# A hybrid encoder step on one core: attention's PSUM banks given to the dense products, the last mixer's products reordered, one projection moved from step 20 to step 15

## The chip, the cores and the metric

The kernel runs on one core of one Trainium2 chip. The metric is the device time of that core in microseconds (us). The kernel before takes 3145.21 us, the median of three runs (3145.02 to 3149.61). The profiled execution that all rows below come from took 3148.22 us, of which the program's span is 3146.1 us.

## The reference

One inference step of a two-layer trunk with width 1024: layer 0 has a recurrent mixer, layer 1 has chunk-band softmax attention, and both have a SwiGLU channel mixer behind their layer norm. There are 1088 rows of activations (1024 of the prompt, 64 of a running stream). What matters here is the end of layer 1:

```python
def layer_norm(x, w, b):
    xf = x.astype(F32)
    mu = jnp.mean(xf, -1, keepdims=True)
    var = jnp.mean(jnp.square(xf - mu), -1, keepdims=True)
    return ((xf - mu) * lax.rsqrt(var + LN_EPS) * w.astype(F32) + b.astype(F32)).astype(x.dtype)

def swiglu(x, w_in, w_out):
    gate, up = jnp.split(x @ w_in, 2, axis=-1)
    return (jax.nn.silu(gate) * up) @ w_out
```

Attention gives a head's output from softmax(q k + bias) v, where each row reads its own chunk of 64 rows and the eight chunks before it. Its output goes through a projection, is added to the residual, normalised, and goes through `swiglu` with 2816 hidden columns.

## The kernel before, in words

**Two halves.** The activations are kept as half A (448 columns) and half B (640 columns, done as two times 320). In the last stage of layer 1 three pieces of work overlap: half B's attention, half A's channel mixer, and, after both, half B's output projection and half B's channel mixer, which ends the program.

**Products.** Everything is float32, made on TensorE (PE) from halves: each operand is split into a high part (`xh`, `wh`) and a low part (`xl`, `wl`), and each product is three matmuls (`wh` by `xh`, `wh` by `xl`, `wl` by `xh`; lines L122 to L124 with the weights stationary, L133 to L136 the other way round). A weight tile of 128x1024 is loaded to `wr`; ScalarE (ACT) makes `wh` (L99), and the low part is made in pieces on VectorE (DVE, L104) and GpSimd (POOL, L106).

**PSUM.** PSUM has eight banks here. `bank` (L138) hands out the three that dense products use, as `gps`. From the start of attention, five others belong to the pool `atps`: two for the scores (`sps`, one buffer of two banks) and three with the tag `t` for attention's transposed probabilities (`tp`), its output (`op`) and the layer norm's transposes (`tps`). The pool is held to the end of the program.

**Half B's attention** goes by pairs of heads; a head has five tiles of 128 rows, in a group of three and a group of two. For one tile: scores on PE (L1262, L1263), add of the bias with the row maximum on DVE (L1266), its negation (L1270), exponential on ACT (L1271), reciprocal on DVE (L1272), scaling on POOL (L1273), four or five transposes on PE (L1278), split of the transposed tile by ACT (L1288) and DVE (L1289). After a group, `op` is accumulated on PE (L1304) and joined (L1308, L1309). The buffer `s` that goes from L1266 to L1278 exists twice.

**Half A's mixer** is a generator `f` of 22 steps. A step loads two weight tiles (gate and up), makes two products of 24 matmuls 448 wide, and forms the hidden tile `ht` and its split `hh`, `hl`. After steps 4, 8, 12, 16, 18 and 22 the products with the second weights (512 wide) are added to the residual `acc`. In program order, each of the last six pairs of attention is followed by two steps of `f`; then comes the rest of `f`, into which half B's projection (`proj`, `layer_norm` and `s_operands`, which forms the sums below) is put at step `JM`.

**Half B's mixer** (`s_ffn`) uses seven products of 12 matmuls, 320 wide, for what would be eight: with the operand's quarters A11, A12, A22 and sums S1 to S4, and the weights' B11, B21, B22 and sums T1 to T4. `s_weights` makes the weights' sums on POOL (L1019 to L1024) and splits them on ACT (L1013) and DVE (L1014). The products run from L1039 to L1041; the 22 steps have three PSUM banks in turn, `pa`, `pb` and `pc`.

**Order of the work.** The code is written in program order, and a scheduler then places the instructions on five engine queues, each of which runs in order. It moves work across program order wherever buffers and inputs allow.

Of the kernel before, what the change touches and what calls it, by code (L numbers as in the profile page):

```python
# [9 lines left out]
F32 = mybir.dt.float32  # L10
# [3 lines left out]
ALU = mybir.AluOpType  # L14
PS = bass.MemoryType.PSUM
# [67 lines left out]
class Kern:  # L83
    def __init__(self, ctx, tc, a):
        self.ctx, self.tc, self.nc, self.a = ctx, tc, tc.nc, a
        self.V, self.A, self.G, self.T = self.nc.vector, self.nc.scalar, self.nc.gpsimd, self.nc.tensor
        self.wcount = 0
        self.both = False
        self.paired = False

# [45 lines left out]
                self.T.matmul(ps, cols(lo(kt)), wh, start=False, stop=(i == n - 1))  # L136

    def bank(self):  # L138
        return self.gp.tile([128, 512], F32, tag="g", name="gps", bufs=3)

    def banks(self, hf):
# [886 lines left out]
    def s_ffn(self, layer, acc, x, hp, hidden, turn, after):  # L1028

        V, A, G, T = self.V, self.A, self.G, self.T  # L1030
        hs, done = {}, 0
        for j in range(NHT):
            B = self.s_weights(j, layer, turn)
            pa, pb, pc = (self.bank()[:, :320] for _ in range(3))

            def product(ps, xn, bn, first):
                (xh, xl), (wh, wl) = x[xn], B[bn]
                for kt in range(4):
                    T.matmul(ps, wh[:, kt, :], xh[:, kt, :], start=(first and kt == 0), stop=False, skip_group_check=True)  # L1039
                    T.matmul(ps, wh[:, kt, :], xl[:, kt, :], start=False, stop=False, skip_group_check=True)  # L1040
                    T.matmul(ps, wl[:, kt, :], xh[:, kt, :], start=False, stop=(kt == 3), skip_group_check=True)  # L1041

            def tmp(n, w=320):
                return hp.tile([128, w], F32, tag=n, name=n, bufs=2)

            t = tmp("ht", 640)
            t1, t2 = t[:, :320], t[:, 320:]
            product(pa, "A11", "B11", True)
            c1 = tmp("c1")
            A.copy(c1, pa)  # L1050
            product(pb, "S2", "T2", True)
            c2 = tmp("c2")
            V.tensor_tensor(c2, pb, c1, op=ALU.add)
            product(pc, "S1", "T1", True)
            product(pb, "S3", "T3", False)
            c3 = tmp("c3")
            V.tensor_tensor(c3, pb, c1, op=ALU.add)
            V.tensor_tensor(c3, pc, c3, op=ALU.add)
            product(pa, "A12", "B21", False)
            A.activation(t1, pa, AF.Tanh, scale=0.5)  # L1060
            V.scalar_tensor_tensor(t1, t1, 1.0, pa, op0=ALU.add, op1=ALU.mult)
            product(pc, "S4", "B22", False)
            V.tensor_tensor(c2, pc, c2, op=ALU.add)
            G.tensor_tensor(t1, t1, c2, op=ALU.mult)
            product(pb, "A22", "T4", False)
            V.tensor_tensor(c1, pb, c1, op=ALU.add)
            A.activation(t2, c1, AF.Tanh, scale=0.5)
            V.scalar_tensor_tensor(t2, t2, 1.0, c1, op0=ALU.add, op1=ALU.mult)
            G.tensor_tensor(t2, t2, c3, op=ALU.mult)
            hh, hl = hidden(j)  # L1070
            A.activation(hh, t, AF.Copy, scale=0.5)
            V.scalar_tensor_tensor(hl, t, 0.5, hh.bitcast(F32), op0=ALU.mult, op1=ALU.subtract)
            hs[j] = hh, hl
            end = j + 1
            if end in self.GROUPS:
                self.tsg(1, acc, lambda nh, pr: self.a["w_fo"][layer, nh, pr], range(done // 2, end // 2),
                         lambda kt: hs[kt][0], lambda kt: hs[kt][1], done == 0, after() if end == NHT else None)
                for i in range(done, end):
                    del hs[i]
                done = end  # L1080
# [235 lines left out]
    def run(self):  # L1316
        nc, tc, a = self.nc, self.tc, self.a
# [2 lines left out]
        self.gla_d = self.dp.tile([2, 128, 128], F32, name="gla_d", tag="gla_d")  # L1320
        self.JX = 6
        self.PB, self.QB, self.turn, self.AQ = 1, 2, 0, (1, 4)
        self.HB, self.PRE, self.JO, self.JM = 5, 4, 16, 20
        es_scan, es_one, es_ps = ExitStack(), ExitStack(), ExitStack()
        self.sp_ps = es_ps.enter_context(tc.tile_pool(name="scps", bufs=1, space=PS))
        self.tpsum = lambda: self.sbank("tps")
# [34 lines left out]
        pa = es_a.enter_context(tc.tile_pool(name="accA", bufs=1))  # L1361
# [46 lines left out]
                    acc1 = self.load_acc(1, a["x"], accp)  # L1408
                self.qk(0, hp, qp, 2)
        es_ps.close()  # L1410
        self.at_ps = self.ctx.enter_context(tc.tile_pool(name="atps", bufs=1, space=PS))
        self.tpsum = lambda: self.at_ps.tile([128, 512], F32, tag="t", name="tps", bufs=3)
        self.proj(1, acc1, "w_om", self.layer_norm(1, acc1, "ln1", 0))
        with tc.tile_pool(name="at0", bufs=1, side="right") as atp:
# [15 lines left out]
        with tc.tile_pool(name="at1", bufs=1, side="right") as atp:  # L1430
# [16 lines left out]
            for hp in range(len(self.AQ), 8):  # L1447
                self.attention(1, hp, atp, parts)
                for _ in range(2):
                    next(f)  # L1450
        for j in f:
            if j == self.JM:
                accp = self.ctx.enter_context(tc.tile_pool(name="accB1", bufs=1, side="right"))
# [97 lines left out]
```

## Time and profile before

| What | Value |
|---|---|
| runs | 3145.21 us (3145.02 to 3149.61) |
| profiled execution | 3148.22 us, span 3146.1 us, mean granted PE clock 0.978 |
| PE busy | 3012.1 us (96%) |
| DVE, ACT, POOL busy | 2026.2, 1264.6, 1331.3 us (64, 40, 42%) |
| longest single wait of PE after 2394.5 us | 22.3 us, on L1039 for L975 |
| last 21 attention tiles and the dense products between them | 2394.5 to 2544.0 us |
| rest of half A's mixer, half B's projection | 2544.0 to 2684.3 us |
| half B's mixer | 2684.3 to 3115.0 us |

Rows of the timeline begin with start and duration in us, then engine, line and operation, `out<-in` by the program's names; a number in brackets is the idle time before it and what ended it. Rows of stretches give the length, then busy us and instructions for PE, PE's weight loads, DVE, ACT and POOL, then the granted PE clock, the DMA share and GB/s. Matmuls are pipelined, so the duration of one is about twice the distance from start to start of a run of them; below, matmuls are priced by that distance.

### The profile page before, as it was taken

The page shows a single profiled execution, that of the slowest core. Times are in us where ns is not written, and L with a number is a line of the kernel's source. Part 1 is how long each engine was busy: PE and PEld are TensorE (multiplying, and loading weights), DVE is VectorE, ACT ScalarE, POOL GpSimd, SP SyncE. Part 2 cuts the span into 40 slices and gives each one's busy share as a digit, 9 for nine tenths or more (in the row PEclk, how much of TensorE's full clock was granted, in tenths as well). Part 3 has the DMA queues.
Part 4 walks back from the last instruction along what each step waited for, and adds up shares of the span by engine and source line. Part 5 has one row for each costly group of instructions (what it writes and reads, how often), then busy time and mean ns, then how long its engine had stood idle before and what let it go on. Part 6 is the DMA issues. An engine that isn't in the chain of part 4 may idle for free.

```text
span 3146.1 us, 50008 instructions
## 1 busy us (share of the span) xinstructions
PE 3012.1 (96%) x17468; PEld 2670.6 (85%) x17468; DVE 2026.2 (64%) x4953; ACT 1264.6 (40%) x2753; POOL 1331.3 (42%) x1461
## 2 busy tenths in 40 slices
PE   9989999899999999999999999999999997899998
PEld 7778888688888877888999898899999886798887
DVE  4677885879898664365553556245666659666557
ACT  4454554344445324244342223355444433333322
POOL 2354533445555234343342323244545535445444
PEclk9989999889999999999999999999999998999999
DMA  6553444534533248434333234765545342222122
GB/s 201 142 155 113 111 113 118 149 103 113 142 105 110 84 131 268 153 111 126 115 110 97 74 101 138 239 184 162 148 141 151 115 145 99 86 68 94 63 72 74
DMA packets 297339, 395.09 MB, mean 126 GB/s; under 512 B 125376, under 2 KB 218424, under 8 KB 297088
## 3 DMA queue, kind: packets, MB, share of 16 engines
q1 hardware_dynamic: 297088, 391.90, 41.8%
q8 instruction: 138, 2.26, 0.3%
q14 instruction: 113, 0.93, 0.1%
HBM read 319.44 MB, written 75.51 MB: 126 GB/s over the span
## 4 chain that ended last, share of the span: by engine, by line
PE 73%; DVE 12%; DMA 7%; issue 3%; ACT 2%; POOL 2%; SPq 1%; POOLq 0%; DVEq 0%; ACTq 0%
PE gps L122 11%; PE gps L123 11%; PE gps L124 11%; PE gps L133 7%; PE gps L134 7%; PE gps L136 6%; PE gps L1039 2%; PE op L1304 2%; PE gps L1040 2%; PE gps L1041 2%; PE tp L1278 2%; DVE t L543 1%; DVE wl L104 1%; DVE x L545 1%; PE sps L1262 1%
## 5 line engine op out<-in xcount | busy, mean ns | idle before, releaser
L106 POOL TENSOR_TENSOR wl<-wr,wh 128x512 fp32r<-128x512 f32 (+2 forms) x289 | 506.0, 1755 | 626.5 <-ACT wh L99 580.5
L122 PE MATMUL gps<-xh,wh 128*128 128x320 f32 (+1 forms) x2188 | 748.4, 342 | 10.2 <-ACT xh L209 5.7
L123 PE MATMUL gps<-xl,wh 128*128 128x320 f32 (+1 forms) x2188 | 747.2, 341 | 0.6 <-DVE xl L210 0.6
L124 PE MATMUL gps<-xh,wl 128*128 128x320 f32 (+1 forms) x2188 | 744.1, 340 | 0.7 <-DVE wl L104 0.7
L99 ACT CAST wh<-wr 128x1024 fp32r<-128x1024 f32 x352 | 366.9, 1048 | 458.5 <-PE gps L123 140.8
L122 PEld LDWEIGHTS gps<-xh,wh 128*128 128x128 f32 x2188 | 415.3, 190 | 32.0 <-ACT wh L99 6.0
L104 DVE TENSOR_TENSOR wl<-wr,wh 128x512 fp32r<-128x512 f32 (+2 forms) x289 | 284.5, 985 | 244.0 <-ACT wh L99 239.4
L123 PEld LDWEIGHTS gps<-xl,wh 128*128 128x128 f32 x2188 | 415.2, 190 | 18.7 <-DVE xl L210 1.0
L124 PEld LDWEIGHTS gps<-xh,wl 128*128 128x128 f32 x2188 | 414.9, 190 | 18.4 <-DVE wl L104 1.1
L1273 POOL TENSOR_SCALAR s<-s,mx 128x640 f32<-128x640 f32 (+5 forms) x144 | 203.4, 1413 | 289.9 <-DVE mx L1272 250.0
L133 PE MATMUL gps<-wh,xh 128*128 128x512 f32 x661 | 262.6, 401 | 10.9 <-DVE acc L816 4.0
L136 PE MATMUL gps<-wh,xl 128*128 128x512 f32 x661 | 259.5, 398 | 4.8 <-DVE xl L210 4.8
L134 PE MATMUL gps<-wl,xh 128*128 128x512 f32 x661 | 261.7, 398 | 2.0 <-DVE wl L104 2.0
L133 PE MATMUL gps<-wh,hh 128*128 128x512 f32 x572 | 226.5, 397 | 2.7 <-DVE acc L818 1.4
L134 PE MATMUL gps<-wl,hh 128*128 128x512 f32 x572 | 225.4, 396 | 0.0
L818 DVE TENSOR_TENSOR acc<-acc,gps 128x512 f32<-128x512 f32 (+1 forms) x216 | 144.7, 679 | 85.3 <-PE gps L136 79.8
L136 PE MATMUL gps<-wh,hl 128*128 128x512 f32 x484 | 188.8, 396 | 2.2 <-DVE hl L924 2.2
L543 DVE TENSOR_TENSOR t<-lt,x 16x48 f32<-16x48 f32 (+9 forms) x540 | 151.6, 281 | 38.6 <-DMA lt<-l_d 28.2
L1271 ACT ACTIVATE s<-s,mx 128x640 f32<-128x640 f32 (+5 forms) x144 | 96.5, 670 | 178.6 <-DVE mx L1270 173.3
L133 PEld LDWEIGHTS gps<-wh,xh 128*128 128x128 f32 x661 | 125.0, 189 | 44.6 <-DVE acc L816 4.8
L136 PEld LDWEIGHTS gps<-wh,xl 128*128 128x128 f32 x661 | 125.1, 189 | 32.9 <-DVE xl L210 5.3
L545 DVE TENSOR_TENSOR x<-x,t 16x48 f32<-16x48 f32 (+9 forms) x540 | 144.0, 267 | 10.9
(351 smaller groups left out, 6291.8 us busy)
## 6 DMA issues: line engine op xcount, KB each, us to landing
wr<-in_w_fi SPq DMA_DIRECT2D x176, 512.0 KB
wr<-in_w_fo SPq DMA_DIRECT2D x88, 512.0 KB
wr<-in_w_in SPq DMA_DIRECT2D x44, 512.0 KB
wr<-in_w_qk SPq DMA_DIRECT2D x32, 512.0 KB
qs<-qd SPq DMA_DIRECT2D x32, 320.0 KB
wr<-in_w_om SPq DMA_DIRECT2D x16, 512.0 KB
wr<-in_w_v SPq DMA_DIRECT2D x16, 512.0 KB
vd<-vh SPq DMA_DIRECT2D x16, 512.0 KB
```

The lines of the kernel that those rows point to most:

```text
L99: self.A.copy(hi, raw)
L104: self.V.tensor_tensor(lo[:, :h], raw[:, :h], hi[:, :h].bitcast(F32), op=ALU.subtract)
L106: self.G.tensor_tensor(lo[:, h:], raw[:, h:], hi[:, h:].bitcast(F32), op=ALU.subtract)
L122: self.T.matmul(ps, hi[:, kt, :], xh, start=(kt == 0), stop=False)
L123: self.T.matmul(ps, hi[:, kt, :], xl, start=False, stop=False)
L124: self.T.matmul(ps, lo[:, kt, :], xh, start=False, stop=(kt == nk - 1))
L133: self.T.matmul(ps, xh, wh, start=(i == 0), stop=False)
L134: self.T.matmul(ps, xh, wl, start=False, stop=(lo is None and i == n - 1))
L136: self.T.matmul(ps, cols(lo(kt)), wh, start=False, stop=(i == n - 1))
L543: V.tensor_tensor(tv, lt[:, j, w:16].unsqueeze(2).to_broadcast([m, r, w]), x[:, 0, j, 0:w].unsqueeze(1).to_broadcast([m, r, w]), op=ALU.mult)
L545: V.tensor_tensor(x[:, 0, w:16, 0:w], x[:, 0, w:16, 0:w], tv, op=ALU.add)
L1273: G.tensor_scalar(s[:m, :nk], s[:m, :nk], mx[:m, 3:4], None, op0=ALU.mult)
```

## The change

It has three parts. After the last attention, `atps` is closed and its five banks are opened as a second pool for `bank`, which then alternates three tiles of the old pool with five of the new one; the transposes of the layer norm (`tpsum`) take `bank` too. In `s_ffn` a fourth bank `pd` is used, S2·T2 is written ahead of A11·B11, S3·T3 and A22·T4 go to `pd`, and the sums `c1`, `c2`, `c3` are formed in another order (one copy and five additions per step, as before). `JM` goes from 20 to 15. Line numbers after the change are higher by 1 from `bank` on, and by 5 behind it.

```diff
@@ -84,7 +84,8 @@
     def __init__(self, ctx, tc, a):
         self.ctx, self.tc, self.nc, self.a = ctx, tc, tc.nc, a
         self.V, self.A, self.G, self.T = self.nc.vector, self.nc.scalar, self.nc.gpsimd, self.nc.tensor
-        self.wcount = 0
+        self.wcount = self.bcount = 0
+        self.gp2 = None
         self.both = False
         self.paired = False
 
@@ -136,6 +137,10 @@
                 self.T.matmul(ps, cols(lo(kt)), wh, start=False, stop=(i == n - 1))
 
     def bank(self):
+
+        self.bcount += 1
+        if self.gp2 and self.bcount % 8 > 2:
+            return self.gp2.tile([128, 512], F32, tag="g2", name="gps", bufs=5)
         return self.gp.tile([128, 512], F32, tag="g", name="gps", bufs=3)
 
     def banks(self, hf):
@@ -1031,7 +1036,7 @@
         hs, done = {}, 0
         for j in range(NHT):
             B = self.s_weights(j, layer, turn)
-            pa, pb, pc = (self.bank()[:, :320] for _ in range(3))
+            pa, pb, pc, pd = (self.bank()[:, :320] for _ in range(4))
 
             def product(ps, xn, bn, first):
                 (xh, xl), (wh, wl) = x[xn], B[bn]
@@ -1045,25 +1050,23 @@
 
             t = tmp("ht", 640)
             t1, t2 = t[:, :320], t[:, 320:]
+            c1, c2, c3 = tmp("c1"), tmp("c2"), tmp("c3")
+            product(pb, "S2", "T2", True)
+            A.copy(c1, pb)
             product(pa, "A11", "B11", True)
-            c1 = tmp("c1")
-            A.copy(c1, pa)
-            product(pb, "S2", "T2", True)
-            c2 = tmp("c2")
-            V.tensor_tensor(c2, pb, c1, op=ALU.add)
+            V.tensor_tensor(c1, pa, c1, op=ALU.add)
             product(pc, "S1", "T1", True)
-            product(pb, "S3", "T3", False)
-            c3 = tmp("c3")
-            V.tensor_tensor(c3, pb, c1, op=ALU.add)
-            V.tensor_tensor(c3, pc, c3, op=ALU.add)
+            V.tensor_tensor(c3, pc, c1, op=ALU.add)
+            product(pd, "S3", "T3", True)
+            V.tensor_tensor(c3, pd, c3, op=ALU.add)
             product(pa, "A12", "B21", False)
             A.activation(t1, pa, AF.Tanh, scale=0.5)
             V.scalar_tensor_tensor(t1, t1, 1.0, pa, op0=ALU.add, op1=ALU.mult)
             product(pc, "S4", "B22", False)
-            V.tensor_tensor(c2, pc, c2, op=ALU.add)
+            V.tensor_tensor(c2, pc, c1, op=ALU.add)
             G.tensor_tensor(t1, t1, c2, op=ALU.mult)
-            product(pb, "A22", "T4", False)
-            V.tensor_tensor(c1, pb, c1, op=ALU.add)
+            product(pd, "A22", "T4", False)
+            V.tensor_tensor(c1, pd, c1, op=ALU.add)
             A.activation(t2, c1, AF.Tanh, scale=0.5)
             V.scalar_tensor_tensor(t2, t2, 1.0, c1, op0=ALU.add, op1=ALU.mult)
             G.tensor_tensor(t2, t2, c3, op=ALU.mult)
@@ -1320,7 +1323,7 @@
         self.gla_d = self.dp.tile([2, 128, 128], F32, name="gla_d", tag="gla_d")
         self.JX = 6
         self.PB, self.QB, self.turn, self.AQ = 1, 2, 0, (1, 4)
-        self.HB, self.PRE, self.JO, self.JM = 5, 4, 16, 20
+        self.HB, self.PRE, self.JO, self.JM = 5, 4, 16, 15
         es_scan, es_one, es_ps = ExitStack(), ExitStack(), ExitStack()
         self.sp_ps = es_ps.enter_context(tc.tile_pool(name="scps", bufs=1, space=PS))
         self.tpsum = lambda: self.sbank("tps")
@@ -1408,7 +1411,8 @@
                     acc1 = self.load_acc(1, a["x"], accp)
                 self.qk(0, hp, qp, 2)
         es_ps.close()
-        self.at_ps = self.ctx.enter_context(tc.tile_pool(name="atps", bufs=1, space=PS))
+        es_at = ExitStack()
+        self.at_ps = es_at.enter_context(tc.tile_pool(name="atps", bufs=1, space=PS))
         self.tpsum = lambda: self.at_ps.tile([128, 512], F32, tag="t", name="tps", bufs=3)
         self.proj(1, acc1, "w_om", self.layer_norm(1, acc1, "ln1", 0))
         with tc.tile_pool(name="at0", bufs=1, side="right") as atp:
@@ -1448,6 +1452,9 @@
                 self.attention(1, hp, atp, parts)
                 for _ in range(2):
                     next(f)
+        es_at.close()
+        self.gp2 = self.ctx.enter_context(tc.tile_pool(name="gp2", bufs=1, space=PS))
+        self.tpsum = self.bank
         for j in f:
             if j == self.JM:
                 accp = self.ctx.enter_context(tc.tile_pool(name="accB1", bufs=1, side="right"))
```

The number of instructions on PE (15089 rows), DVE, POOL and SP stays the same. The order of the queues is the same up to the first row shown here. In the following, `gps` is a dense product, `tp`, `sps` and `op` belong to attention; the number behind a name tells buffers apart.

**PE, where the last 21 attention tiles begin.** Before:

```order
L124 MATMUL gps_27101<-xh0_69,wl_27090 128x448
L122 MATMUL gps_27101<-xh0_69,wh_27089 128x448
L1278 MATMUL tp_25674<-ident_71,s_25667 128x128 x4
L1278 MATMUL tp_25681<-ident_71,s_25667 128x128
L123 MATMUL gps_27101<-xl0_70,wh_27089 128x448
L1262 MATMUL sps_25724<-ks_25611,qs_25612 128x320
L1263 MATMUL sps_25724<-ks_25611,qs_25612 128x320
```

Now:

```order
L134 MATMUL gps_27075<-wh_27028,hh_26947 128x512
L135 MATMUL gps_27075<-wl_27029,hh_26947 128x512
L1281 MATMUL tp_25674<-ident_71,s_25667 128x128 x4
L1281 MATMUL tp_25681<-ident_71,s_25667 128x128
L1265 MATMUL sps_25724<-ks_25611,qs_25612 128x320
L1266 MATMUL sps_25724<-ks_25611,qs_25612 128x320
```

Before, dense products of half A's step 12 (counted from 0) stand between the pieces of an attention tile, and so on for the next 760 rows. Now the attention tiles follow one another with no dense product in between.

**PE, where those attention tiles end.** Now:

```order
L1307 MATMUL op_26789<-xh1_23955,vt_26498 128x128
L1307 MATMUL op_26789<-xl1_23956,vt_26498 128x128
L123 MATMUL gps_27105<-xh0_69,wh_27093 128x448
L124 MATMUL gps_27105<-xl0_70,wh_27093 128x448
L125 MATMUL gps_27105<-xh0_69,wl_27094 128x448
```

The dense product `gps_27105` is the one that before was `gps_27101`, in the rows above. It now stands behind the last `op` of attention, and with it everything of half A's steps 12 to 21. Behind it come steps 12 to 15 and their second weights, then half B's projection, then step 16.

**DVE, where half B's normalised rows are made.** These are residual rows `acc`, their splits `xl1`, the sums S2 to S4, and the low half `wl` of half A's next weights. Before:

```order
L818 TENSOR_TENSOR acc_28001<-acc_28001,gps_28440 128x512
L982 TENSOR_TENSOR ss_28331<-sc_28330,st_28332 128x256
L866 BN_STATS bs_28454<-acc_28001 128x6
L104 TENSOR_TENSOR wl_28596<-wr_28593,wh_28595 128x640
L988 TENSOR_TENSOR sc_28330<-tps_28314,sc_28330 128x256
```

Now:

```order
L113 TENSOR_TENSOR xl1_27521<-gps_28028,xh1_27520 128x4x64
L997 TENSOR_TENSOR ss_28045<-gps_28035,ss_28045 128x256
L980 TENSOR_TENSOR st_28120<-xh1_27520,xl1_27521 128x256
L105 TENSOR_TENSOR wl_28159<-wr_28156,wh_28158 128x640
L823 TENSOR_TENSOR acc_27566<-acc_27566,gps_28065 128x512
```

Before, the weight between these rows was that of step 20; now it is that of step 16, 71 DVE rows behind the first finished residual row of half B. The same chain of layer norm and sums stands ahead of it.

**PE, where half B's mixer begins.** Before:

```order
L134 MATMUL gps_28834<-wl_28693,hh_28661 128x512
L884 MATMUL tps_28548<-ident_71,acc_28003 128x128 x4
L1039 MATMUL gps_28887<-xh1_27957,wh_28867 128x320
L1040 MATMUL gps_28887<-xl1_27958,wh_28867 128x320
L1041 MATMUL gps_28887<-xh1_27957,wl_28868 128x320
```

Now:

```order
L134 MATMUL gps_28838<-wh_28696,hh_28665 128x512
L135 MATMUL gps_28838<-wl_28697,hh_28665 128x512
L1044 MATMUL gps_28892<-S2h_27574,wh_28882 128x320
L1045 MATMUL gps_28892<-S2l_27575,wh_28882 128x320
L1044 MATMUL gps_28891<-xh1_27520,wh_28871 128x320
L1045 MATMUL gps_28891<-xl1_27521,wh_28871 128x320
L1046 MATMUL gps_28891<-xh1_27520,wl_28872 128x320
```

Before, its first product took A11 (`xh1`, `xl1`) with B11. Now the first two matmuls are those of S2 with T2's high half, and A11's follow.

## The prediction

> **What bounds the kernel now.** I read the page's busy shares first, then stretches of the end, where all of the change lies (up to 2394.5 us the queues are the same), then PE's waits there.
>
> ```profile
> PE 3012.1 (96%) x17468; PEld 2670.6 (85%) x17468; DVE 2026.2 (64%) x4953; ACT 1264.6 (40%) x2753; POOL 1331.3 (42%) x1461
> ```
>
> PE is busy 96% of the span, so a gain can only come out of its pauses, and any new pause is a loss. The stretches are, in turn: the last 21 attention tiles of half B with dense products between them; the rest of half A's mixer and half B's projection; the hole ahead of half B's mixer; and that mixer.
>
> ```profile
> 2394.50:2544.00 149.50, 149.50 (x833) 136.61 (x832) 95.47 (x215) 70.76 (x135) 74.95 (x55) 1.00 0.44 126
> 2544.00:2661.50 117.50, 106.76 (x480) 87.44 (x480) 91.19 (x150) 40.15 (x68) 47.68 (x41) 0.97 0.37 129
> 2661.50:2684.30 22.80, 0.55 (x3) 0.15 (x2) 21.55 (x34) 6.23 (x15) 13.62 (x10) 0.50 0.48 149
> 2684.30:3115.00 430.70, 411.80 (x2400) 378.04 (x2400) 262.85 (x333) 142.08 (x191) 201.27 (x146) 0.99 0.22 74
> ```
>
> The first stretch has no pause at all: PE is busy for 149.5 of 149.5 us at full clock. The second loses 10.7 us and about 3.5 us more to the clock (3% of 117.5). The third is a hole of 22.3 us, with DVE busy throughout. The mixer loses 18.9 us, and 4.3 us to the clock (1% of 430.7). PE's waits from 2544 us to the end name these losses:
>
> ```profile
> PE gps L1039 <- DVE st L975: 22.3, 1, 22.3
> PE gps L1041 <- DVE wl L1014: 6.1, 6, 2.7
> PE gps L1039 <- DVE ht L1061: 4.3, 5, 1.2
> PE gps L133 <- DVE acc L816: 4.0, 2, 3.3
> PE gps L133 <- DVE acc L818: 3.1, 6, 1.1
> PE gps L1039 <- DVE c L1057: 2.1, 4, 0.6
> ```
>
> The hole is the wait for half B's sums (L975). The waits for `ht`, `acc` and `c` are waits for a bank to be read out, and `wl` is a late weight.
>
> **What the change can take away.** With the projection at step 15, half B's rows, norm and sums are made while PE still has steps 16 to 21, so the hole goes: 22.3 us. The 10.7 us and 3.5 us of the stretch ahead go with it at most, since they come from the same chain on DVE: together **-36**. Eight banks instead of three take the bank waits: 4.3 + 4.0 + 3.1 + 2.1 = 13.5 us, **-14**; the mixer's 4.3 us of clock, most of it the restart behind the hole, **-4**. Sum: -54 us.
>
> **What it adds, first: attention without cover.** The order shows it plainly: the last 21 tiles now follow one another, and the dense products that stood between them come behind. Five of the eight banks that these products use exist only once attention's are given back. So the first stretch is taken apart into dense products and attention; the first takes PE as long as before, the second as long as attention takes alone. PE's part of the dense work, from one of its groups in that stretch and two neighbouring starts of each width:
>
> ```profile
> L123 PE MATMUL gps<-xl,wh 128*128 128x448 f32 x131 | 48.4, 369 | 0.0
> ...
> 2496.15 0.36 PE L124 MATMUL gps<-xh,wl 128*128 128x448 f32 x1
> 2496.35 0.36 PE L122 MATMUL gps<-xh,wh 128*128 128x448 f32 x1
> ...
> 2514.31 0.39 PE L134 MATMUL gps<-wl,hh 128*128 128x512 f32 x1
> 2514.54 0.39 PE L136 MATMUL gps<-wh,hl 128*128 128x512 f32 x1
> ```
>
> The quoted line's 131 matmuls go with as many on L122 and on L124: 393 at 0.20 us from start to start are 80 us. The 512-wide ones are 132 in the order of these rows: at 0.23 us 30 us. So 110 us of the 149.5 are dense and **39.5 us are attention** on PE. How long it takes alone no row shows, so I bound it. One tile's chain, as it ran elsewhere, with its transposes from another tile:
>
> ```profile
> 2033.36 0.81 DVE L1266 CUSTOM_DVE_ANT_0 s<-sps,bias 128x640 f32<-128x640 f32 x1
> ...
> 2034.41 0.83 ACT L1271 ACTIVATE s<-s,mx 128x640 f32<-128x640 f32 x1 [1.49 <-DVE mx L1270]
> 2035.62 1.89 POOL L1273 TENSOR_SCALAR s<-s,mx 128x640 f32<-128x640 f32 x1 [3.56 <-DVE mx L1272]
> ...
> 2493.99 0.71 PE L1278 MATMUL tp<-ident,s 128*128 128x128 f32 x5
> ```
>
> From the start of the sum to the end of POOL's scaling are 2037.51 - 2033.36 = 4.15 us; the five transposes add 0.71, and the buffer `s` can be written again only behind them. With the steps from engine to engine and the queueing of a second tile on the same engines I take 6.2 us for a round. There are two buffers, so 3.1 us per tile. Two rows of an earlier head, where two tiles ran close, agree:
>
> ```profile
> 2070.44 0.81 DVE L1266 CUSTOM_DVE_ANT_0 s<-sps,bias 128x640 f32<-128x640 f32 x1
> ...
> 2073.47 0.82 DVE L1266 CUSTOM_DVE_ANT_0 s<-sps,bias 128x640 f32<-128x640 f32 x1 [0.28 <-PE tp L1278]
> ```
>
> That is 3.03 us. A head of five tiles is then 15.5 us, and about 2 us where a group ends, since `op` waits for the last split and the next scores stand behind it: 17.5 us. Four heads are 70 us, the twenty-first tile and the last output about 11 us, and a late bias about 5 us, for its load took 9.7 us from issue to use, and POOL's copy now stands ahead of a tile's scaling:
>
> ```profile
> 2401.03 0.65 SPq L1240 DMA_DIRECT2D bias<-bias_d  x1
> ...
> 2410.75 0.51 POOL L1241 COPY bias<-bias 128x384 f32<-128x384 f32 x1 [6.60 <-DMA bias<-bias_d]
> ```
>
> The matmuls that remain are sparse, so I add about 7 us for stretches at half clock (the third stretch above has it at 0.50). That makes 93 us, against 39.5 on PE when covered: **+54**. The lower bound is the busiest other engine without any waiting. Its attention groups in the stretch:
>
> ```profile
> L1289 DVE TENSOR_TENSOR xl<-tp,xh 128x512 fp32r<-128x512 f32 x23 | 15.8, 686 | 1.3 <-ACT xh L1288 1.2
> ...
> L1266 DVE CUSTOM_DVE_ANT_0 s<-sps,bias 128x640 f32<-128x640 f32 x17 | 13.9, 818 | 4.8 <-POOL s L1273 2.1 <-POOL wl L106 1.5 <-PE sps L1263 1.2
> ```
>
> These two are 29.7 us; DVE's smaller groups of attention in that stretch bring it to about 50, so not under +11. The upper bound is the present pace: all of 149.5 us, +110. I take the chain because it is the only one of the three with each step priced, and give it 42 to 68.
>
> **What it adds, second: three waits on weights.** Half B's projection is now followed by step 16, whose low half of the weights stands 71 DVE rows behind the first finished residual row; before, a stretch of 74 such rows ran from
>
> ```profile
> 2588.92 0.69 DVE L818 TENSOR_TENSOR acc<-acc,gps 128x512 f32<-128x512 f32 x1 [0.68 <-PE gps L136]
> ...
> 2634.71 0.41 DVE L112 TENSOR_TENSOR xl<-ss,xh 128x256 fp32r<-128x256 f32 x1
> ```
>
> in 45.8 us, with other work among it. Without that I take 40 us. PE has about ten projection products of 12 matmuls left (0.23 us each, 28 us), so it waits about **+12**; bounds 0 (DVE keeps up) and 18. At the start of half B's mixer S2·T2 comes first, and T2 is the last but one of the weights to be formed: POOL's and DVE's rows were
>
> ```profile
> 2652.78 1.69 DVE L1014 TENSOR_TENSOR wl<-wr,wh 128x1024 fp32r<-128x1024 f32 x1
> ...
> 2660.45 1.25 DVE L1014 TENSOR_TENSOR wl<-wr,wh 128x1024 fp32r<-128x1024 f32 x1
> ```
>
> 7.7 us from B11's split to T2's, and their buffers are held until half A's last products: **+7** (0 if they come early, 10 with the load). Later steps start with T2 as well; the 6.1 us of late `wl` may become 10: **+4**. Two restarts at half clock in place of one: **+2**. The edits to `c1` to `c3` are as many operations on the same engines, under products of 12 matmuls: nothing, and 22 times 0.3 us, 7 us, if that cover is gone.
>
> **The sum.** 54 + 12 + 7 + 4 + 2 - 54 = +25 against the profiled 3148.2 us, so about 3173 there. Two of the terms taken away may be larger: a bank waits also where a late start shows only as a slow matmul; I allow 3 us, which gives +22. The median of the runs is 3.0 us below the profiled one, so I forecast **3167 us**. With attention's 42 to 68 that is 3155 to 3181, and the terms for weights give 8 us more on either side.
>
> [...]
>
> **Rivals.** *Attention runs at its engines' pace.* Then it takes 50 us of DVE and about 10 to fill and drain, +21 instead of +54, if DVE, ACT and POOL overlap neighbouring tiles better than two buffers let me think: 3167 - 33 = 3134 us, faster. For it: no engine but DVE comes over 45 us. Against it: the buffer `s` exists twice, and its round is over 5 us without any queueing. It decides from about +30 downward. Chance 0.17.
>
> *No net change.* Attention costs about +38 and everything else stands: 3151 us, or 3145 with the projection's wait hidden. Chance 0.13.
>
> *Half clock through all of attention.* An earlier stretch with short pauses shows what this means:
>
> ```profile
> 613.00:647.00 34.00, 30.98 (x141) 24.86 (x142) 29.38 (x89) 16.41 (x47) 21.77 (x33) 0.50 0.34 107
> ```
>
> At 0.50 PE gives 141 matmuls in 34 us, 4.1 per us, and looks 91% busy; the mixer, at 0.99, gives 2400 in 430.7 us, 5.6 per us. Attention's 39.5 us then cost up to 79, partly under the chain; 104 us instead of 93, or with the weight chain at its bound, 3178 to 3188. [...] Against it: scores and outputs come in bursts. Chance 0.24. [...]
>
> *The dense products still run between.* Then only the removals count and the time would be about 3110. The order of rows speaks against it; 0.02, counted with the first rival.
>
> **The numbers.** Forecast 0.44, first rival with the last 0.19, no change 0.13, half clock 0.24. This kernel's measurement tells 0.2%, 6.3 us, from no change. Of the forecast's part nearly all, and all of half clock, is slower: 0.68. Faster 0.19, same 0.13. The range reaches into the first rival and to half clock's upper end: 3134 to 3190; the slower cases alone have 3153 to 3190.
>
> **What would show it.** Right: a stretch of about 90 us with 240 matmul rows of attention alone, its tiles 3 to 3.5 us apart and PE idle over half; no hole ahead of half B's mixer; a pause of 8 to 15 us at step 16 and of about 7 us on S2·T2; `ht` and `c` gone from the mixer's waits. Wrong: tiles 2.5 us apart (first rival), PE clock at 0.5 throughout attention (third), or a hole that has only moved.

## The result: slower by 1.5%, twice what was forecast

The changed kernel takes 3195.1 us (median of four runs, 3191.79 to 3199.22); the kernel before, with a further run, 3147.41 us. The ratio is 1.0151, with a 95% interval from 1.0133 to 1.0169: about 48 us more, where 22 were forecast, and 5 us above the upper end of the range. The profiled execution took 3194.15 us, its span is 3192.4 us.

The page's first line on the engines:

```profile
PE 3038.5 (95%) x17468; PEld 2695.8 (84%) x17468; DVE 2029.7 (64%) x4953; ACT 1263.7 (40%) x2753; POOL 1342.5 (42%) x1461
```

PE does the same 17468 operations in 26 us more of busy time, while the mean granted clock fell from 0.978 to 0.968; PE's share of the span fell by a point. The stretches of the changed kernel, as the view of busy time by stretch gives them (length, then busy us of PE, its weight loads, DVE, ACT and POOL, then the granted PE clock, DMA share, GB/s): attention alone; the dense products of steps 12 to 15; the projection up to the last transposes; steps 16 to 21; the pause ahead of half B's mixer; the mixer.

```profile
2394.50:2486.00 91.50, 67.36 (x309) 55.66 (x307) 46.81 (x142) 41.21 (x97) 44.81 (x33) 0.73 0.33 85
2486.00:2549.10 63.10, 62.19 (x282) 54.69 (x282) 31.30 (x39) 20.76 (x28) 23.98 (x14) 0.95 0.49 172
2549.10:2654.00 104.90, 75.32 (x300) 60.67 (x300) 60.22 (x109) 23.42 (x45) 29.85 (x25) 0.84 0.19 61
2654.00:2738.30 84.30, 84.30 (x402) 75.28 (x401) 54.34 (x87) 26.63 (x41) 26.33 (x20) 1.00 0.30 96
2738.30:2749.70 11.40, 0.41 (x3) 0.02 (x1) 10.13 (x15) 2.81 (x3) 8.65 (x6) 0.63 0.32 122
2749.70:3160.00 410.30, 404.84 (x2421) 380.83 (x2422) 268.18 (x338) 144.09 (x195) 217.00 (x155) 0.99 0.26 85
```

Attention's 307 matmuls now have 91.5 us for themselves, at a mean clock of 0.73; under cover they took 39.5 us of PE. That is 52 us lost, and 54 were forecast. The mixer takes 410.3 us instead of 430.7. The surprise is the third stretch: 104.9 us with PE idle for 29.6. PE's waits behind attention (total us, times, longest):

```profile
PE gps L889 <- POOL acc L882: 13.1, 2, 7.2
PE gps L1044 <- ACT wh L1018: 12.4, 2, 11.0
PE gps L889 <- DVE acc L884: 12.0, 2, 7.6
PE gps L889 <- issue: 4.4, 1, 4.4
```

L889 is the layer norm's transposes (L884 before). They wait 13.1 + 12.0 + 4.4 = 29.5 us for the normalised rows, in five pauses, one per row tile of half B; no such row stands in the waits before. The hole of 22.3 us for half B's sums is gone, as forecast, and in its place stands a pause of 11 us for T2's weights (L1018).

The timeline of PE at the first of the five pauses (start, duration):

```profile
2582.51 0.40 PE L137 MATMUL gps<-wh,xl 128*128 128x512 f32 x1
2587.32 0.84 PE L889 MATMUL gps<-ident,acc 128*128 128x128 f32 x4 [4.41 <-DVE acc L884]
2587.81 0.78 PE L134 MATMUL gps<-wh,xh 128*128 128x512 f32 x1
2588.38 0.63 PE L135 MATMUL gps<-wl,xh 128*128 128x512 f32 x1
2588.81 0.63 PE L137 MATMUL gps<-wh,xl 128*128 128x512 f32 x1
```

The projection's next products (L134 on) stand behind the transposes in the same queue and wait with them (the first starts 0.49 us behind L889), although they could be done before, as the experiments below show. What the transposes wait for is the layer norm of the row tile that PE has just finished, one operation after the other (start, duration, from the chain of waits):

```profile
2582.67 0.25 PE gps L137
2582.94 0.70 DVE acc L823
2583.66 0.70 DVE bs L871
2584.70 0.75 POOL rstd L875
2585.52 0.96 POOL rstd L876
2586.51 0.76 DVE acc L884
2587.32 0.84 PE gps L889 x4
```

PE also comes back slow: the products start 0.43 us apart (2588.38 to 2588.81), where 0.23 us is their distance at full clock; the granted clock is 0.55 from 2587.32 to 2591.14 us and 1.00 from 2560 to the pause. Counted by the distance from start to start of PE's instructions, each against the usual one of its shape, the stretch from 2560 to 2665 us loses 41.6 us: the 29.5 us of pauses and 12 us at the slower clock behind them. The same count gives 71 us for the kernel before from 2394 us to the end and 116 us for the changed one, 45 us more, which is the result within 2 us.

| lost on PE, us | before | changed |
|---|---|---|
| attention's last 21 tiles | 0 | 52.7 |
| from there to half B's mixer | 10.2 | 54.7 |
| first 25 us of the mixer (with the hole, before) | 29.4 | 4.2 |
| rest of the mixer and the tail | 31.9 | 4.6 |

What attention loses in the experiments is counted in the same way, and has the projection's wait for attention's output in it.

### The profile page after: what moved, and what is told of

It is laid out like the page before. It is cut to its first block, busy times and chain, and to the rows that moved or that the text cites. A ratio compares the mean times of both kernels' runs of the same rounds, so it can differ in the third digit from the quotient of the medians.

```text
span 3192.4 us, 50089 instructions
## 1 busy us (share of the span) xinstructions
PE 3038.5 (95%) x17468; PEld 2695.8 (84%) x17468; DVE 2029.7 (64%) x4953; ACT 1263.7 (40%) x2753; POOL 1342.5 (42%) x1461
## 4 chain that ended last, share of the span: by engine, by line
PE 76%; DVE 9%; DMA 6%; issue 4%; POOL 3%; ACT 2%; SPq 1%; POOLq 0%; DVEq 0%; ACTq 0%
PE gps L123 11%; PE gps L124 11%; PE gps L125 11%; PE gps L134 7%; PE gps L135 7%; PE gps L137 6%; PE gps L1044 2%; PE gps L1045 2%; PE gps L1046 2%; PE op L1307 2%; PE tp L1281 2%; DVE x L550 1%; PE sps L1265 1%; DVE t L548 1%; PE ps L621 1%
## 5 line engine op out<-in xcount | busy, mean ns | idle before, releaser
L107 POOL TENSOR_TENSOR wl<-wr,wh 128x384 fp32r<-128x384 f32 (+2 forms) x289 | 510.7, 1771 | 690.3 <-ACT wh L100 632.6
L105 DVE TENSOR_TENSOR wl<-wr,wh 128x640 fp32r<-128x640 f32 (+2 forms) x289 | 284.0, 983 | 257.7 <-ACT wh L100 255.6
L125 PEld LDWEIGHTS gps<-xh,wl 128*128 128x128 f32 x2188 | 416.4, 190 | 20.5 <-DVE wl L105 1.5
L124 PEld LDWEIGHTS gps<-xl,wh 128*128 128x128 f32 x2188 | 416.6, 190 | 18.5 <-DVE xl L215 1.0
L134 PE MATMUL gps<-wh,xh 128*128 128x512 f32 x661 | 263.1, 403 | 2.9 <-ACT xh L1074 2.5
L137 PE MATMUL gps<-wh,xl 128*128 128x512 f32 x661 | 260.9, 401 | 4.8 <-DVE xl L215 4.8
L134 PE MATMUL gps<-wh,hh 128*128 128x512 f32 x572 | 226.6, 397 | 0.3 <-DVE acc L823 0.3
L137 PE MATMUL gps<-wh,hl 128*128 128x512 f32 x484 | 189.4, 397 | 2.8 <-DVE hl L929 2.8
L137 PEld LDWEIGHTS gps<-wh,xl 128*128 128x128 f32 x661 | 126.1, 191 | 32.5 <-DVE xl L215 5.3
L134 PEld LDWEIGHTS gps<-wh,xh 128*128 128x128 f32 x661 | 126.5, 192 | 31.9 <-ACT xh L1074 2.9
```

Of the source, the lines that this page charges most:

```text
L105: self.V.tensor_tensor(lo[:, :h], raw[:, :h], hi[:, :h].bitcast(F32), op=ALU.subtract)
L107: self.G.tensor_tensor(lo[:, h:], raw[:, h:], hi[:, h:].bitcast(F32), op=ALU.subtract)
L124: self.T.matmul(ps, hi[:, kt, :], xl, start=False, stop=False)
L125: self.T.matmul(ps, lo[:, kt, :], xh, start=False, stop=(kt == nk - 1))
L134: self.T.matmul(ps, xh, wh, start=(i == 0), stop=False)
```

## The experiments

Every kernel is timed against the kernel before, run beside it on the same chip; its medians there were 3151.3 (first four), 3149.6 (next four) and 3151.8 us (last four).

**Theory and rivals.** At first I held that both losses come from the banks (theory "banks"): attention loses its cover because the dense products must wait for its banks, and the transposes, now tiles of the same two pools, hold the dense products back. The rival was that the pauses are the price of doing the layer norm at step 15, whatever the banks.

### The change without the move to step 15

```diff
-        self.HB, self.PRE, self.JO, self.JM = 5, 4, 16, 15
+        self.HB, self.PRE, self.JO, self.JM = 5, 4, 16, 20
```

> The change with the projection left at step 20. Theory (banks): what the change lost is attention without cover (+53 us) and the layer norm's transposes, which now share the eight banks with the dense products and so hold them back in PE's queue (42 us of pauses); both come from the banks and not from the step, so both stay, and the hole ahead of half B's mixer is partly back: 3195 to 3220 us, at least 30 us of waits before L889. Rival (step): the pauses came with the move to step 15; then they are gone, and only attention's 53 us against about 15 us saved in the mixer remain: 3165 to 3185 us.

Measured: 3175.0 us, ratio 1.0081 (1.0062 to 1.0101). Attention loses 52.6 us, as expected. The time lies in the rival's range, and the pauses are nearly gone, as the rival said; the hole is partly back, as the theory said:

```profile
PE gps L1044 <- ACT S3h L112: 14.8, 1, 14.8
PE gps L889 <- POOL acc L882: 6.7, 4, 3.2
```

The transposes share the pools here too, so sharing alone doesn't make 29.5 us of pauses: my theory fell in this form. Putting the order of PE's queue beside it shows a difference. In the change, 144 matmuls of the projection stand ahead of the first transposes; here 168 do, 24 more, which are the two products of one more row tile. So the question became what lets the projection run ahead.

### Only the move to step 15

The one line above, in the kernel before (20 to 15).

> Only the projection moved to step 15, with the banks and the mixer as before. Theory (banks): no long pause at the layer norm's transposes, since dense products of steps 16 and 17 stand between them; the hole of 22.3 us gone; but only the steps up to 15 can cover attention, and 147 of its 307 matmuls are left without cover, about half of 53 us. 3145 + 25 - 31 + 5 to 15 = 3144 to 3154 us. Rival (step): pauses of about 42 us at the layer norm as in the change: 3175 to 3185 us.

Measured: 3167.1 us, ratio 1.0050 (1.0033 to 1.0067), between the two. There are no pauses before the transposes, 198 projection matmuls stand ahead of the first, and products of steps 16 and 17 stand between the next ones. So the move alone doesn't make the pauses. But the scheduler can hoist only steps 12 to 15 among the attention tiles (the projection's own tiles come next), and attention loses 31.1 us. Of the hole's 22 us and what lies around it, part returns as waits for weights at the mixer's start (13.4 us lost in its first 25 us). The move is a loss by itself.

### The change with banks of their own for the transposes

```diff
-        if self.gp2 and self.bcount % 8 > 2:
-            return self.gp2.tile([128, 512], F32, tag="g2", name="gps", bufs=5)
+        if self.gp2 and self.bcount % 5 > 2:
+            return self.gp2.tile([128, 512], F32, tag="g2", name="gps", bufs=2)
...
-        self.tpsum = self.bank
+        self.tpsum = lambda: self.gp2.tile([128, 512], F32, tag="t2", name="tps", bufs=3)
```

> The change, but of the five freed banks three serve the transposes alone and two go to the dense products. Theory (banks): the waits before L889 shrink from 42 us to 5 to 15 us, since products of step 16 can now stand between the transposes; attention also gets about 22 us of dense cover, since the first dense tiles come from the old three banks: 3140 to 3160 us. Rival (late chain): DVE, POOL and ACT are too slow for half B's normalisation whatever the banks, and the 42 us show up at step 16 or 17: 3170 to 3185 us.

Measured: 3168.6 us, ratio 1.0056 (1.0036 to 1.0075): 27 us less than the change. The waits before L889 are gone but for one of 0.8 us (the largest rows of its waits behind attention):

```profile
PE gps L1044 <- ACT wh L1018: 11.4, 2, 11.0
PE gps L134 <- ACT xh L1074: 4.5, 1, 4.5
PE gps L123 <- DVE ht L919: 3.5, 1, 3.5
```

The stretch from the projection to the mixer loses 15.4 us instead of 52.3, and 11 of them are T2's pause. The layer norm is thus not too slow for step 15. The time lies above the theory's range (3140 to 3160 us) all the same. The expected gain in attention was wrong: 72 dense matmuls did get among its tiles, but it still loses 49.7 us. They are worth 15 us of cover and stand among the first tiles only: 269 of attention's matmuls come behind the last of them, and those lose 49 us.

### The change with the two pools' alternation shifted

The second theory: the tiles of one pool are given out in the order of the program, and `bank` sends the requests to the two pools by their number. Counted in the code, the first row tile's transposes are requests 527 and 528 and the next row tile's products 529 and 530. With the rule "remainder by 8 above 2: new pool", 527 goes to the new pool and 528, 529 and 530 to the old one. By this theory the next tile's products stand behind one of these transposes in their pool, and cannot go ahead of it. With the step at 20 the same transposes are requests 545 and 546, both in the old pool, and the next tile's products 547 and 548, both in the new one: the theory has these products free, and 168 matmuls are what PE's queue shows there. A shift of the remainder changes no work and no step; it does move every later request for a bank too, those of half A's last steps and of half B's mixer among them.

```diff
-        if self.gp2 and self.bcount % 8 > 2:
+        if self.gp2 and (self.bcount + 1) % 8 > 2:
```

> The change with the alternation of the two pools shifted by one: every bank request goes where the next one went before. Attention stays without cover, so 53 us stay. Theory (ring order): in the change, half of a row tile's transposes share a pool with the next tile's products, and since the tiles of a pool are given out in program order those products must wait for the layer norm; after the shift both transposes of a tile lie in one pool and the next tile's products in the other, so the 42 us of pauses between the projection and step 16 shrink to 5 to 12 us: 3195 - 33 = 3162 us, 3155 to 3170. Rival (late chain): the pauses are the layer norm's length at step 15 and stay, 3190 to 3200 us.

Measured: 3185.8 us, ratio 1.0114 (1.0097 to 1.0131), between the two expected ranges. I had described the shift too kindly: both transposes now lie in the old pool, but so does one of the next tile's two products (529), so 156 matmuls stand ahead, not 168. With a shift of two, 527 and 528 lie in the old pool and 529 and 530 in the new one:

> The change with the alternation of the pools shifted by two instead of one. Now 168 projection matmuls stand ahead of the first transposes on PE, as at step 20, against 144 in the change and 156 with a shift of one; 72 dense matmuls also get among the attention tiles. Theory (ring order sets how far the projection may run ahead of the layer norm, and the pauses follow that lead): waits before L889 of 5 to 12 us instead of 42, attention's lost time 45 to 50 instead of 52.7: 3155 to 3165 us. Rival (step 15 itself): pauses of 20 us or more whatever the lead: 3170 to 3182 us.

Measured: 3164.6 us, ratio 1.0044 (1.0030 to 1.0059). The waits of the shift by one, and by two:

```profile
PE gps L889 <- POOL acc L882: 20.7, 4, 6.9
```

```profile
PE gps L889 <- POOL acc L882: 6.6, 3, 3.3
PE gps L1044 <- ACT wh L1018: 6.1, 1, 6.1
```

Together:

| kernel | projection matmuls ahead of the first transposes | waits before the transposes, us |
|---|---|---|
| the change | 144 | 29.5 |
| shift by one | 156 | 20.7 |
| shift by two | 168 | 6.6 |
| step 20 | 168 | 6.7 |
| own banks for the transposes | 198 | 0.8 |

One number in one expression takes away 23 of 29.5 us, and each time the matmuls ahead are the number that the requests' pools give. That shows the mechanism: the pauses come from the order that two kinds of work are forced into by sharing a pool. The times hold more than the pauses, since the shift moves other banks as well: with a shift of two, attention still loses about 50 us, T2's pause falls to 6.1 us, and the first 25 us of the mixer lose about 17 us in place of 4.

### The hand-over written just ahead of the projection

The three lines that close `atps` and open the new pool are moved into the loop, to the start of step 15's branch; nothing else differs from the change.

> The change with the hand-over of the five banks written just ahead of the projection instead of straight behind attention. The steps 12 to 14 and the second weights can then cover attention as with step 15 alone; the alternation, the projection and the mixer stay as in the change. Attention's lost time 31 us instead of 52.7, the pauses of 42 us and the 11 us on S2 stay: 3195 - 22 = 3173 us, 3168 to 3178. If the covered work only moves the pauses elsewhere, above 3185 us.

Measured: 3177.8 us, ratio 1.0082 (1.0067 to 1.0097). Attention loses 32.2 us instead of 52.7, 7.0 of them in the projection's wait for attention's output; the five pauses and T2's are those of the change. So 20 us of attention's loss come from where the hand-over is written, the rest from the step, since only steps 12 to 15 can be hoisted (with the step alone moved, 31.1 us). The time falls by 17 us, or by 22 us with each kernel set against the kernel before that ran beside it.

### Three buffers for the scores in place of two

```diff
+            es_3 = ExitStack()
+            self.sp3 = es_3.enter_context(tc.tile_pool(name="s3", bufs=1))
...
-                    s = sp.tile([128, bw], F32, tag="s", name="s", bufs=self.QB)
+                    s = (self.sp3 or sp).tile([128, bw], F32, tag="s", name="s", bufs=3 if self.sp3 else self.QB)
```

> The change with three buffers s in place of two for half B's attention behind the first two head pairs. 231 of attention's matmuls are then without cover instead of 307. If the two buffers set the pace of uncovered tiles (3.9 us each in the change), three bring a tile to 2.9 to 3.3 us, attention's lost time falls from 52.7 to about 30: 3195 - 22 = 3173 us. If the one pair of score banks or the chain sets it, a tile stays at 3.6 to 3.9 us, and the lost time falls only with the number of uncovered matmuls, to 40: 3182 us.

Measured: 3165.2 us, ratio 1.0040 (1.0026 to 1.0055), better than either expected. The tile's first DVE operation (L1266 before; lines behind `s_ffn` are higher by 3, not by 5), in the change and here (minimum, median and maximum in ns, first and last start):

```profile
L1269 DVE CUSTOM_DVE_ANT_0 s<-sps,bias x22: 672/824/826, 2393.1 to 2474.4; 128x640 f32<-128x640 f32 x18, 128x512 f32<-128x512 f32 x4
```

```profile
L1269 DVE CUSTOM_DVE_ANT_0 s<-sps,bias x17: 673/815/825, 2393.5 to 2446.6; 128x640 f32<-128x640 f32 x14, 128x512 f32<-128x512 f32 x3
```

In the change 21 intervals take 81.3 us, 3.87 us a tile; with three buffers 16 intervals take 53.1 us, 3.32 us. In the change this operation waits for a tile's transposes to free its buffer (from DVE's waits):

```profile
DVE s L1269 <- PE tp L1281: 9.8, 10, 3.1
```

With three buffers no such wait is left. The two buffers were the tighter limit, as the prediction held; and with a third the scheduler had more tiles done before, so fewer stayed uncovered. Attention loses 22.4 us. Fewer uncovered matmuls alone don't give this: the shift by two leaves 250 of them without cover and loses 43 us there, this kernel 231 and loses 22. How much of the better pace is the clock isn't settled, since it is 0.94 here over attention's last 60.5 us and 0.73 in the change.

### Late banks: a version that keeps attention's cover

The hand-over is put behind half A's mixer, so that the dense products of half A keep their own three banks, and the transposes attention's; only half B's mixer gets eight.

```diff
-        es_at.close()
-        self.gp2 = self.ctx.enter_context(tc.tile_pool(name="gp2", bufs=1, space=PS))
-        self.tpsum = self.bank
         for j in f:
...
         es_a.close()
+        es_at.close()
+        self.gp2 = self.ctx.enter_context(tc.tile_pool(name="gp2", bufs=1, space=PS))
+        self.tpsum = self.bank
```

Four kernels have this, with the step at 18, 19 or 20, and at 18 with the old order of the mixer's products.

> The five banks are handed over only when half A's mixer is done, and the projection stands at step 18; the mixer's new order stays. Theory (banks): attention is covered but for its last 34 matmuls (+3 to +8 us), no long pauses at the layer norm, no hole of 22 us, S2 first costs about 11 to 14 us at the start of half B's mixer, and the mixer itself keeps its saving of about 23 us: 3145 + 5 - 32 - 5 + 14 - 23 = about 3104 us, 3095 to 3115. Rival (step): moving the projection costs a pause of its own, 20 us or more: above 3120 us.

> As the run with late banks and step 18, with step 19. Twelve of attention's matmuls instead of 34 are left without cover, at most 8 us less there; one step less stands behind the projection to hide the layer norm and the sums, 20 us less of cover. Theory: attention 11.4 us of lost time becomes 4, and the chain is still hidden: 3108 us, 3102 to 3114. Rival: the chain comes out at the mixer's start, a hole of 5 to 15 us: 3115 to 3125 us.

> As the run with late banks, with the projection left at step 20: only the banks and the mixer's order differ from the kernel before. Attention fully covered, the 22 us hole ahead of the mixer stays, the mixer keeps 23 us less of bank waits, and S2·T2 first costs nothing beside the hole: 3145 - 23 = 3122 us, 3117 to 3130. If the banks' gain in the mixer is offset by the start: 3130 to 3140 us.

> As the run with late banks and step 18, but with the old order of the mixer's products (A11·B11 first, three banks of the eight per step). If starting on S2·T2 is a loss, the 10.6 us pause goes and 3 to 6 us of weight waits take its place: 3108 us, 3103 to 3112. If the reordering pays (fewer waits for c and ht in each of 22 steps, 0.3 to 0.6 us a step), it is slower: 3118 to 3125 us.

| late banks | time, us | ratio (interval) | attention loses | first pause of the mixer |
|---|---|---|---|---|
| step 18 | 3114.6 | 0.9882 (0.9864 to 0.9900) | 11.4 | 10.6 |
| step 19 | 3122.1 | 0.9915 (0.9900 to 0.9930) | 10.4 | 20.5 |
| step 20 | 3129.9 | 0.9941 (0.9927 to 0.9956) | 0.3 | 32.9 |
| step 18, old order | 3128.6 | 0.9933 (0.9918 to 0.9948) | 11.5 | several, 1.4 to 3.1 |

The run at step 20 and the first experiment, also at step 20, differ only in where the hand-over is written: 3129.9 us late, 3175.0 us early. Of what attention loses at step 18, most is the projection's one wait for attention's output (10.2 us of it at step 19):

```profile
PE gps L134 <- ACT xh L214: 6.7, 1, 6.7
```

The first waits at the mixer with step 18, and with step 20:

```profile
PE gps L1044 <- ACT wh L1018: 10.6, 1, 10.6
```

```profile
PE gps L1044 <- ACT S2h L112: 32.9, 1, 32.9
```

At step 20 the hole is longer than before the change (32.9 against 22.3 us, in the slowest of its four executions, 3138.0 us), because S2·T2 now comes first and S2 is among the last sums to be made; I had thought this start free. At step 19 the rival was right in its time and too low with its hole of 5 to 15 us: 20.5 us of the chain come out at the mixer's start, and attention loses 10.4 us where 4 were expected. At step 18 the chain is hidden and T2's weights end last. The reordering, of which I thought mainly the price at the start, pays: with the old order the kernel is slower by 14 us (16 with each set against the kernel before beside it), since waits like these are spread over the mixer:

```profile
PE gps L1046 <- DVE wl L1019: 5.6, 7, 1.9
PE gps L134 <- ACT xh L1076: 5.2, 1, 5.2
PE gps L1044 <- DVE c L1062: 4.7, 3, 3.0
```

The last run joins late banks, step 18 and the third buffer:

> Late banks and step 18, with the third buffer s: all of attention's matmuls have dense ones around them, and 92 dense matmuls stand behind the last of them, over the 6.7 us that the projection waited for attention's output. Lost time of attention 11.4 us to about 1; the 10.6 us on S2 stay: 3114 - 10 = 3104 us, 3100 to 3108. If the pauses only move, 3111 to 3118 us.

Measured: 3104.0 us, ratio 0.9849 (0.9834 to 0.9864): the fastest version here, 48 us under the kernel before where the change was 48 us over. Its first stretches:

```profile
2394.50:2544.00 149.50, 147.36 (x780) 131.90 (x779) 91.39 (x189) 66.05 (x120) 71.41 (x49) 0.99 0.47 153
2544.00:2652.00 108.00, 101.24 (x474) 85.01 (x472) 89.62 (x166) 38.51 (x70) 40.86 (x37) 1.00 0.26 88
2652.00:2664.00 12.00, 7.36 (x35) 7.36 (x36) 11.94 (x14) 2.81 (x3) 10.85 (x8) 0.60 0.56 179
2664.00:3076.00 412.00, 405.64 (x2412) 378.90 (x2411) 266.20 (x338) 142.84 (x194) 211.29 (x152) 1.00 0.25 82
```

Attention is covered again (2.1 us idle of 149.5), the stretch with the projection has 6.8 us idle of 108, and the mixer is as short as in the change (412.0 us against 430.7). T2's pause of 10.6 us is still there.

## Why the prediction was right in its direction and wrong in its size

**Attention without cover (+54): right.** 91.5 us for attention alone, against 93 in the working, and 52.7 us lost. The two buffers limit it as argued, and the clock is lower (0.73 on the mean). The pace of 3.87 us a tile lies between the working's 3.5 us and the 4.1 us that its 12 us for the late bias and for half clock make of it over 20 tiles.

**What the change takes away (-54): right in kind, too small, in other shares.** The hole went. By the count of lost time PE had 71.5 us to lose and keeps 10.9 besides attention, the five pauses and T2's, so 61 us were taken away. The working's 54 also holds 4.4 us twice: of the waits for `acc`, 3.3 and 1.1 us lie in the stretch ahead of the hole, whose 10.7 us were counted whole. The mixer gave back more than the 18 us set down for banks and clock: what PE loses behind its first 25 us fell from 31.9 to 4.6 us, 27 us. The old order with late banks still loses 18.5 us there, against 3.8 with the new one, so about half of this is the reordering, which the prediction costed at nothing.

**The wait behind the projection (+12): the step that failed.** It priced one wait, that of step 16 for its weights, by setting 40 us of work on DVE against 28 us on PE, as if all of PE's products could be done while the chain ran. What stood in PE's queue was a tile's products, then its transposes, then the next tile's products: five times the latency of the layer norm of one tile, in series, 4.4 to 7.6 us each, and slow products behind each. That is 41.6 us in place of 12, and the 29.6 us between them are more than the whole miss of about 26; the 7 us more that were taken away made up for part. In PE's queue L889 stands right behind L137, with no product between; the prediction looked there only at the row of step 16. The wait that it priced is hardly there: behind the last tile PE goes on with step 16's products at once. The weights cost about 2 us inside the fifth pause, where their low half stands on DVE between two operations of the last tile's layer norm:

```profile
2639.68 0.69 DVE L871 BATCH_NORM_STATS2 bs<-acc 128x6 f32<-128x512 f32 x1
2641.47 0.83 DVE L105 TENSOR_TENSOR wl<-wr,wh 128x640 fp32r<-128x640 f32 x1 [1.09 <-ACT wh L100]
2642.21 0.20 DVE L873 BATCH_NORM_AGGREGATE mv<-bs 128x2 f32<-128x12 f32 x1
```


**T2 first (+7), T2's later waits (+4), restarts (+2): near.** T2's pause is 11.0 us, just above the bound of 10, later waits for weights 1.4 us in place of 4, and the start of the mixer loses 4.2 us more.

**The rivals.** The engines' pace in attention didn't come. Half clock through all of attention would have been 104 us; it was 91.5, with the clock at 0.59 to 0.84 over stretches of 20 to 25.5 us: in part. Which of attention's matmuls or pauses bring the clock down no run shows; the chance of 0.24 was my estimate. None of the rivals was the five pauses; "a hole that has only moved" was named among the signs of a wrong prediction, without a price.

## What to carry to other kernels

In an in-order queue, as PE's is here (the projection's next products stood behind L889 through its 4.4 us), look for each instruction that waits on a chain started by the instructions just ahead of it, and count what stands between: what matters is not whether there is enough other work in sum, but whether it can be placed in that gap. A pool whose tiles are given out in program order also orders the work that uses it; two kinds of work with different delays want pools of their own, or an alternation chosen so that the quick one isn't put behind the slow one. Banks that one kind of work has finished with are best handed over where the receiver needs them, not at the first place in the program where they are free: here the hand-over itself kept the receiver's work from covering the giver's.

## What the runs showed of the hardware

The first pause, 4.4 us on PE, cost more than its length. Behind it the chain of waits gives (start, duration):

```profile
2588.16 0.43 PE gps L134
...
2590.72 0.43 PE gps L134
2591.14 0.26 PE gps L135
2591.40 0.23 PE gps L137
```

Products of one shape take 0.43 us each until 2591.14 and 0.23 us after, 3.8 us behind the restart at 2587.32; the granted clock over these 3.8 us is 0.55, and 1.00 in the 2.7 us after. Behind the pauses of 7.2 and 7.6 us the slow products lasted 6.0 and 6.1 us. Five pauses of 29.5 us thus cost 41.6 us.

With dense products between them the last 21 attention tiles leave PE no pause (149.5 us busy of 149.5); one after the other they lost 52.7 us. The version that keeps the interleaving and still gives the mixer its banks, with the step at 18, loses 11.4 us there and is 80 us faster than the change, and 91 us with the third buffer.
